# Seven half-size products for the latent tokens in the first layer's feed-forward, and its residual added in DRAM

## The chip, the cores and the metric

The kernel runs on one core of one Trainium2 chip. The metric is the device time of one execution, in microseconds (us); the median over three runs is shown, and one execution was profiled.

## The reference

Two layers work on 512 latent tokens and 256 context tokens of 1024 features, in float32. Layer 0 has retention and mLSTM heads, layer 1 windowed attention. Each layer ends with a gated feed-forward of 2816 hidden columns; in layer 0 it runs for latent and context tokens with the same weights, in layer 1 for latent tokens alone:

```python
def _swiglu(h, w_in, w_out):
    g, u = jnp.split(h @ w_in, 2, axis=-1)
    return (jax.nn.silu(g) * u) @ w_out
...
        x = x + g1 * y
        x = x + g2 * _swiglu(_rmsnorm(x, norm_w[layer, 1]) * (1.0 + sc2) + sh2, ffn_w_in[layer], ffn_w_out[layer])
        if not last:
            ctx = ctx + cg1 * yc
            ctx = ctx + cg2 * _swiglu(_rmsnorm(ctx, norm_w[layer, 1]) * (1.0 + csc2) + csh2,
                                      ffn_w_in[layer], ffn_w_out[layer])
```

The scales, shifts and gates (`sc2`, `sh2`, `g2` and so on) come from the conditioning vector through the matrices `ada_w` (1024 x 6144 per layer).

## The kernel before

**Tiles.** Features lie on the 128 partitions, tokens along the free dimension: the residual stream `xt` is four tiles of two feature tiles by 768 tokens, context tokens 0 to 255 first and latent tokens 256 to 767 after them. A float32 product is made of three matmuls on numbers rounded for the fast path: high times high, high times low, low times high. So each weight tile is split into a high part (a cast on ScalarE) and a low part (a subtraction on VectorE), and each activation too.

**The feed-forward of layer 0** (`op_ffn`, L1505). `inproj` takes column tiles of 128 hidden columns, always one of the gate and one of the up half; I call these two a pair, and there are 22. Each pair needs 2 x 8 x 3 matmuls over the 512 latent tokens and as many over the 256 context tokens. ScalarE applies SiLU to the gate, VectorE multiplies, and the product is split again. After 6, 10, 14 and 18 pairs `outproj` (L1551) multiplies the oldest four with `ffn_w_out`; six are left for the end. Each of its eight output tiles is scaled by the gate and added to `xt` by one VectorE instruction per token part, straight from PSUM. The last group also sums squares for the next norm.

**The feed-forward of layer 1** (`op_ffn_seven`) is another one: the product of a pair is seen as a two by two block product (feature halves by token halves, gate and up as the two output rows) and is done in seven half-size products in place of eight, by sums of weight blocks (`Weights.seven`, L535, on VectorE) and sums of activation blocks (the forms t2, t3, n1, n4, in `norm_seven`); the first two pairs run plain. The results are put together by 256-wide VectorE instructions.

**Order of the work.** The program is written as Python generators. `Flow` (L28) runs them and keeps a rough clock per engine to decide in which order they emit instructions; the tile framework then schedules each engine's queue by that order and by what is ready in its own model. On the chip each queue runs in order. `Weights` (L482) loads weights through SyncE's queue three loads ahead, and splits them when a buffer is free. `ada_stream` (L691) multiplies rows of `ada_w` with the conditioning vector on VectorE (one instruction per row tile of 128 x 1024 and per column: latent, context) beside the main work; its loads stand in SyncE's queue too, in a ring of six buffers (`ada_open`, L738). Seven of these run beside the feed-forward of layer 0, one of them needed by its own output groups.

**Memory.** Nineteen large slots (`big`) are shared by all activations; PSUM has eight banks: two under the tag `mx`, two under `pj`, and two tiles of two banks each (`psum2`). Every instruction goes through the helper in L107, so the profile has one line and groups by tile name: `pg`, `pu` are gate and up products, `pf` outputs, `wr`, `wh`, `wl` weights as loaded, high and low, `aw` and `acc` rows and sums of the modulation.

## Time and profile before

| | us |
|---|---|
| median of 3 runs | 1776.29 (1775.38 to 1778.4) |
| profiled execution | 1777.82 |
| its span | 1776.0 |
| TensorE busy | 1721.4 (97%) |
| VectorE busy | 1136.9 (64%) |
| ScalarE busy | 685.5 (39%) |
| GpSimd busy | 274.6 (15%) |

The span is the time from the first to the last instruction of the profiled execution. The feed-forward of layer 0 lies between about 550 and 1107 us of it, that of layer 1 from about 1411 us to the end. Busy times of TensorE are those of pipelined matmuls, each shown longer than the time by which it moves the next one; the time of a matmul is therefore read from a row of many. The mean granted clock of TensorE was 0.985 of full speed. GpSimd issues no DMA in this kernel.

### The profile page before, as it was taken

To read this page: it belongs to the slowest core of one execution; us is meant where nothing else is said; L and a number is where in the kernel's file an instruction comes from. 1 tells how busy PE (TensorE), PEld (TensorE's weight loads), DVE (VectorE), ACT (ScalarE), POOL (GpSimd) and SP (SyncE) were. 2 spreads that over 40 slices of the span, in tenths; PEclk is the share of its full clock that TensorE was granted. 3 is DMA by queue.
4 is the path that set the end of the run, shared out by engine and by line. 5 is a ranking of instruction groups with operands and counts; after the bars stand their busy time and mean duration, and the time that the engine had idled before them with its cause. 6 is when DMAs were issued, how large, how long until landed. Compare 5 with 4: busy or idle time off the path is not lost.

```text
span 1776.0 us, 29522 instructions
## 1 busy us (share of the span) xinstructions
PE 1721.4 (97%) x11922; PEld 1528.9 (86%) x11922; DVE 1136.9 (64%) x2048; ACT 685.5 (39%) x1346; POOL 274.6 (15%) x271
## 2 busy tenths in 40 slices
PE   6899999999999999999999999898999999999998
PEld 5799899999878888888888888898666989999998
DVE  5845365756597376563544324869886687778785
ACT  4532344433325221212121123545776553444343
POOL 4211120201123000000000002426454300000000
PEclk8999899999999999999999999898999999999999
DMA  9511111011574264443542215322002623333335
GB/s 332 209 52 48 37 37 48 25 38 53 196 239 117 75 186 132 129 148 125 162 134 78 67 37 153 96 61 60 1 1 66 184 72 95 107 96 107 107 88 150
DMA packets 224556, 184.35 MB, mean 104 GB/s; under 512 B 7532, under 2 KB 206628, under 8 KB 224420
## 3 DMA queue, kind: packets, MB, share of 16 engines
q1 hardware_dynamic: 222468, 178.20, 32.9%
q10 hardware_dynamic: 1952, 4.27, 0.7%
q8 instruction: 94, 1.54, 0.4%
q14 instruction: 42, 0.34, 0.1%
HBM read 175.10 MB, written 7.34 MB: 103 GB/s over the span
## 4 chain that ended last, share of the span: by engine, by line
PE 84%; DVE 7%; ACT 3%; issue 3%; DMA 2%; POOL 1%; SPq 0%; POOLq 0%; ACTq 0%; DVEq 0%
PE pf L107 28%; PE pu L107 18%; PE pg L107 14%; PE pt L107 10%; PE sc L107 3%; PE ao L107 2%; PE mo L107 2%; PE atr L107 2%; PE ro L107 1%; DVE acc L107 1%; PE kv L107 1%; DVE wl L107 1%; PE me L107 1%; DMA wr<-in_ab_w_in_dram 1%; DVE hfull L107 1%
## 5 line engine op out<-in xcount | busy, mean ns | idle before, releaser
L107 ACT CAST wh<-wr 128x1024 fp32r<-128x1024 f32 (+1 forms) x186 | 188.2, 1012 | 345.7 <-PE pf L107 165.5
L107 DVE TENSOR_TENSOR wl<-wr,wh 128x1024 fp32r<-128x1024 f32 (+1 forms) x186 | 225.4, 1212 | 105.5 <-ACT wh L107 104.3
L107 POOL TENSOR_TENSOR nacc<-nacc,sq 128x256 f32<-128x256 f32 (+1 forms) x42 | 56.7, 1349 | 630.7 <-ACT sq L107 627.5
L107 DVE SCALAR_TENSOR_TENSOR xt<-pf,mod,xt 128x512 f32<-128x512 f32 (+1 forms) x160 | 97.7, 613 | 84.3 <-PE pf L107 83.8
L107 DVE TENSOR_TENSOR hfull<-pu,sq 128x512 f32<-128x512 f32 (+1 forms) x44 | 24.5, 557 | 149.9 <-PE pu L107 149.6
L107 PE MATMUL pf<-fh,wh 128*128 128x256 f32 (+1 forms) x352 | 119.3, 340 | 0.8 <-ACT wh L107 0.8
L107 PE MATMUL pf<-fl,wh 128*128 128x256 f32 (+1 forms) x352 | 118.5, 337 | 0.0
L107 PE MATMUL pf<-fh,wl 128*128 128x256 f32 (+1 forms) x352 | 118.0, 338 | 0.5 <-DVE wl L107 0.5
L107 PE MATMUL pf<-fu,wh 128*128 128x512 f32 (+1 forms) x448 | 116.2, 349 | 1.1 <-ACT fu L107 0.5
L107 PE MATMUL pu<-hT,wh 128*128 128x256 f32 x640 | 115.4, 280 | 0.0
L107 DVE SCALAR_TENSOR_TENSOR acc<-aw,cmod,acc 128x1024 f32<-128x1024 f32 x90 | 114.8, 1298 | 0.0
L107 PEld LDWEIGHTS pu<-hT,wh 128*128 128x128 f32 x640 | 97.8, 188 | 0.6 <-ACT hT L107 0.2
L107 PE MATMUL pu<-hT,wl 128*128 128x256 f32 x320 | 88.0, 281 | 1.4 <-DVE wl L107 1.4
L107 PE MATMUL pt<-wh,hh 128*128 128x256 f32 x288 | 84.2, 294 | 3.8 <-ACT hh L107 2.6
L107 PEld LDWEIGHTS pf<-fu,wh 128*128 128x128 f32 x448 | 76.8, 188 | 12.6 <-ACT fu L107 0.7
L107 PE MATMUL pt<-wl,hh 128*128 128x256 f32 x288 | 83.7, 292 | 0.0
L107 PE MATMUL pg<-g0h,wh 128*128 128x512 f32 (+1 forms) x220 | 82.1, 373 | 1.5 <-ACT sq L107 1.5
L107 POOL TENSOR_TENSOR aE<-aE,ast 128x512 f32<-128x512 f32 (+1 forms) x64 | 73.0, 1154 | 66.9 <-DVE ast L107 51.5
L107 PE MATMUL pg<-g0l,wh 128*128 128x512 f32 (+1 forms) x220 | 82.3, 374 | 0.0
L107 PE MATMUL pt<-wh,hl 128*128 128x256 f32 x288 | 82.2, 288 | 0.0
L107 PE MATMUL pu<-g0l,wh 128*128 128x512 f32 (+1 forms) x220 | 82.1, 373 | 0.0
L107 PE MATMUL pu<-g0h,wh 128*128 128x512 f32 (+1 forms) x220 | 81.9, 372 | 0.0
(382 smaller groups left out, 5169.2 us busy)
## 6 DMA issues: line engine op xcount, KB each, us to landing
wr<-in_ffn_w_in_dram SPq DMA_DIRECT2D x88, 512.0 KB, 3.9
aw<-in_ada_w_dram SPq DMA_DIRECT2D x84, 512.0 KB, 4.5
wr<-in_ab_w_in_dram SPq DMA_DIRECT2D x32, 512.0 KB, 4.3
wr<-in_ffn_w_out_dram SPq DMA_DIRECT2D x32, 512.0 KB, 4.7
wr<-in_ffn_w_out_dram SPq DMA_DIRECT2D x32, 384.0 KB, 3.6
wr<-in_ab_w_out_dram SPq DMA_DIRECT2D x16, 512.0 KB
wr<-in_attn_w_out_dram SPq DMA_DIRECT2D x16, 512.0 KB, 4.1
aw<-in_ada_w_dram SPq DMA_DIRECT2D x8, 768.0 KB
```

The source lines that it names most:

```text
L107: r = fn(*a, **k)
```

## The change

The latent tokens of 20 of the 22 pairs in layer 0 get the seven half-size products: per pair 7 x 4 x 3 matmuls of 256 columns. The context tokens keep their plain product, 48 matmuls of 256 columns, of which those with the gate stand after the first of the seven products, and those with the up half before the last two; both fill one bank of the tag `mx` (`bank_e`) that is read at the end of the pair. The first two pairs run plain, latent tokens in 256-wide halves. `Weights.seven` gets two more kinds of job: in `all` the up half is split whole and last, after the two sums.

The norm (`norm_seven0`) writes eight float32 tiles first, then splits them into the forms; b21, b12 and b22 wait until the outputs of the mixer are done, t2 to n4 until the context's norm is done. The forms take 12 large slots, so `xt` does not stay in SBUF: it is stored to `xs2` in DRAM, the four inner output groups are scaled by ScalarE into two halves of a staging tile and added in DRAM by accumulating DMAs from GpSimd's queue, and `xt` is loaded again before the last group, which adds in SBUF as before. The groups now run after pairs 4, 8, 12 and 16 counted from 0. The modulation ring has three buffers in place of six, and the modulations stand after every third pair.

```diff
--- before.py
+++ after.py
...
-            yield lambda: self.asked > job[1] and "pool" in F1
+            F = F0 if job[2] in ("all", "eight0") else F1
+            yield lambda: self.asked > job[1] and "pool" in F
...
-            split("u", [t[:, 8:12] for t in x], u[:, 4:8])
-            self.freed += 2
-            self.ask()
-            yield
+            if job[2] == "seven":
+                split("u", [t[:, 8:12] for t in x], u[:, 4:8])
+                self.freed += 2
+                self.ask()
+                yield
             yield spend((self.n_p, 1))
             split("z", whl(), z)
             yield
             yield spend((self.n_p, 1))
             split("y", whl(), y)
+            if job[2] == "all":
+                yield
+                yield spend((self.n_x, 1))
+                split("u", xs_(), u)
+                self.freed += 2
+                self.ask()
...
-        pool_ = ada_ring["ctx"].enter_context(tc.tile_pool(name="aw", bufs=6))
+        pool_ = ada_ring["ctx"].enter_context(tc.tile_pool(name="aw", bufs=3))
-        for _ in range(6):
+        for _ in range(3):
             ada_ask()
...
+        F0["ctx"] = ExitStack()
+        F0["pool"] = F0["ctx"].enter_context(tc.tile_pool(name="f0", bufs=1))
+        F0["rows"], F0["sums"] = 8, 2
...
-    op_out(ab_w_out[0], mixed, 0, 2, (LAT, CTX), op_norm(0, 1, "g0"), (32, 24))
...
+    xs2 = drp.tile([4, P, 2 * NT], F32, name="xs2")
+    ORDER0 = ("b11", "b21", "b22", "", "", "t2", "t3", "n1", "n4")
...
+        for q in range(4):
+            bb.append(big([P, 3, NL], F32, "bb"))
+            for k in range(2):
+                kk = 2 * q + k
+                dve.scalar_tensor_tensor(bb[q][:, k], xk(xt, kk, a, b), amod[0][:, 1, kk, 0:1], bcs, ALU.mult, ALU.mult)
+                act.activation(bb[q][:, k], bb[q][:, k], AF.Identity, bias=mod[0][:, 24 + kk, 0:1])
...
+        for q, (b11, b21, b12, b22, t2) in enumerate(four):
+            two("b11", q, b11)
+        done0.add("b11")
+        yield lambda: "mixed" in done0
+        for name, i in (("b21", 1), ("b12", 2), ("b22", 3)):
+            for q in range(2):
+                two(name, q, four[q][i])
+            done0.add(name)
+            yield
+        yield lambda: 0 in done0
+        for q, (b11, b21, b12, b22, t2) in enumerate(four):
+            dve.tensor_tensor(b11, b11, b12, ALU.subtract)
+            dve.tensor_tensor(t2, b22, b11, ALU.add)
+        for name in ("t2", "t3", "n1", "n4"):
+            for q, (b11, b21, b12, b22, t2) in enumerate(four):
+                if name == "t3":
+                    dve.tensor_tensor(b12, b12, b22, ALU.subtract)
+                if name == "n4":
+                    dve.tensor_tensor(b21, b21, t2, ALU.subtract)
+                two(name, q, {"t2": t2, "t3": b12, "n1": b11, "n4": b21}[name])
+            done0.add(name)
+            yield
...
+    def norms0(part):
+        def run():
+            flow.add(norm_seven0() if part is LAT else norm_ctx0(), 3, "norm")
+            if part is CTX:
+                done0.add("mixed")
+                for kk in range(4):
+                    nc.gpsimd.dma_start(xs2[kk], xt[kk].rearrange("p j n -> p (j n)"))
+        op_do(run)
+
+    op_out(ab_w_out[0], mixed, 0, 2, (LAT, CTX), norms0, (32, 24))
+
...
+        def product(o, w, r0, name, start=True):
+            wh, wl = w
+            pairs = []
+            for k in range(4):
+                h, lo = form0(0, name, k // 2)[:, k % 2], form0(1, name, k // 2)[:, k % 2]
+                pairs += [(wh[:, r0 + k], h), (wh[:, r0 + k], lo), (wl[:, r0 + k], h)]
+            for i, (l_, r_) in enumerate(pairs):
+                pe.matmul(o, l_, r_, start=(start and i == 0), stop=(i == 11), skip_group_check=True)
...
+        def inproj(fi):
             def gen():
-                th, tl = big([P, 2, NT], F32R, "fh"), big([P, 2, NT], F32R, "fl")
-                acts[pr] = th, tl
...
-                for t in range(2):
...
-                        for j in range(2):
-                            if len(u) <= j:
-                                u += yield from W.take(1)
-                                ps.append([bank("pg") for _ in range(2)] if j == 0 else halves_ps(psum2("pu")))
-                            yield from steps(ps[j][i][:, 0:b - a], pairs_feat(u[j], 0, *x_(), a, b), cut=24)
-                            if part is (ends if first else parts)[-1]:
-                                W.give(1)
-                            if j:
-                                evac(t, part, ps[0][i], ps[1][i])
-                            flow.cur.t = 0.0
-                            yield
...
+                acts[fi] = t = big([P, 2, NT], F32R, "fu")
+                u, = yield from W.take(1)
+                keep = F0["pool"].tile([P, NL], F32, tag="keep", name=nm("keep"), bufs=2)
+                u23 = F0["pool"].tile([P, 2, 256], F32, tag="u23", name=nm("u23"), bufs=1)
+                m1 = keep[:, 256:512]
+
+                def context(i):
+                    yield from steps(bank_e[:, 256 * i:256 * i + 256], pairs_feat(u["gu"[i]], 0, ctx0(0), ctx0(1), 0, NCX),
+                                     cut=24)
+
+                bank_a = psum("pg", "mx")[:, 0:256]
+                product(bank_a, u["g"], 0, "b11")
+                act.copy(m1, bank_a)
+                rest()
+                yield
+                bank_e = psum("pc", "mx")
+                yield from context(0)
+                rest()
+                yield
+                product(bank_a, u["g"], 4, "b21", start=False)
+                W.n_x.n += 1
+                act.activation(keep[:, 0:256], bank_a, AF.Silu)
+                rest()
+                yield lambda: "z" in u and "t2" in done0
+                pu = psum2("pu")
+                bank_b, bank_d = pu[:, 0:256], pu[:, 512:768]
+                product(bank_b, u["z"], 0, "t2")
+                dve.tensor_tensor(u23[:, 0], bank_b, m1, ALU.subtract)
+                rest()
+                yield lambda: "y" in u and "t3" in done0
+                product(bank_d, u["y"], 0, "t3")
+                dve.tensor_tensor(u23[:, 1], bank_d, u23[:, 0], ALU.add)
+                rest()
+                yield lambda: "n1" in done0
+                bank_c = bank("pu")[:, 0:256]
+                product(bank_c, u["y"], 4, "n1")
+                W.give(1)
+                cc = t3("hfull")
+                dve.tensor_tensor(cc[:, 256:512], u23[:, 1], bank_c, ALU.subtract)
+                rest()
+                yield lambda: "u" in u
+                yield from context(1)
+                rest()
+                yield lambda: "n4" in done0
+                product(bank_d, u["u"], 4, "n4", start=False)
+                W.n_x.n += 1
+                dve.tensor_tensor(cc[:, 0:256], bank_d, u23[:, 0], ALU.add)
+                rest()
+                yield
+                product(bank_c, u["z"], 4, "b22", start=False)
+                W.give(1)
+                dve.tensor_tensor(m1, bank_c, u23[:, 0], ALU.subtract)
+                act.activation(m1, m1, AF.Silu)
+                dve.tensor_tensor(cc, cc, keep, ALU.mult)
+                act.copy(t[:, 0, NCX:NT], cc)
+                dve.tensor_tensor(t[:, 1, NCX:NT], cc, f(t[:, 0, NCX:NT]), ALU.subtract)
+                rest()
+                yield
+                output(fi, slice(0, NCX), bank_e[:, 0:256], bank_e[:, 256:512])
...
+        def output(fi, c, pg, pu):
...
+            act.activation(sg, pg, AF.Silu)
+            dve.tensor_tensor(cc, pu, sg, ALU.mult)
+            act.copy(t[:, 0, c], cc)
+            dve.tensor_tensor(t[:, 1, c], cc, f(t[:, 0, c]), ALU.subtract)
...
+        def plain():
...
+                for fi in range(PLAIN):
...
+                    for j in range(2):
+                        for r in range(2):
+                            for i, t in enumerate("gu"):
+                                yield lambda: halves[j][r] in done0
+                                product(banks[i][:, 256 * j:256 * j + 256], us[fi][t], 4 * r, halves[j][r], start=r == 0)
...
+                    acts[fi] = big([P, 2, NT], F32R, "fu")
+                    output(fi, slice(NCX, NT), *banks)
+                yield lambda: 0 in done0
...
+        def modulate(fi):
+            if ada and fi % 3 == 0:
                 l_, t0 = ada.pop(0)
-                op_ada(l_, t0, on_pe=(), gap=5.0 if l_ else 2.0, cols=1 if l_ and t0 >= 16 else 2)
+                op_ada(l_, t0, on_pe=(), gap=5.0 if l_ else 1.0, cols=1 if l_ and t0 >= 16 else 2)
...
+        def outproj(fs):
...
+                if not end and len(stage) == 0:
+                    stage.append(big([P, 2, NT], F32, "stage"))
...
                         for part in these:
                             a, b, mc = part
-                            ps = (bank if end and last else wide_bank)("pf")
+                            ps = wide_bank("pf")
                             yield from steps(ps[:, 0:b - a], pairs_feat(u, P * t, bh, bl, a, b, nk))
                             if part is these[-1] and t == ncol // P - 1:
                                 W.give(1)
-                            dve.scalar_tensor_tensor(xk(xt, k, a, b), ps[:, 0:b - a], mod[l][:, 40 + k, mc:mc + 1],
-                                                     xk(xt, k, a, b), ALU.mult, ALU.add)
+                            gate = mod[0][:, 40 + k, mc:mc + 1]
                             if end:
+                                dve.scalar_tensor_tensor(xk(xt, k, a, b), ps[:, 0:b - a], gate, xk(xt, k, a, b),
+                                                         ALU.mult, ALU.add)
+                                square_sum(k, a, b)
+                            else:
+                                act.activation(stage[0][:, k % 2, a:b], ps[:, 0:b - a], AF.Copy, scale=gate)
...
+                        if not end:
+                            nc.gpsimd.dma_start(xs2[k // 2, :, NT * (k % 2):NT * (k % 2) + NT], stage[0][:, k % 2],
+                                                accum_op=ALU.add)
...
             if end:
+                op_do(reload)
...
+        def reload():
+            nonlocal xt
+            xt = [big([P, 2, NT], F32, "xt") for _ in range(4)]
+            for kk in range(4):
+                nc.gpsimd.dma_start(xt[kk].rearrange("p j n -> p (j n)"), xs2[kk])
+
+        for fi in range(NF):
+            if fi >= PLAIN:
+                inproj(fi)
+            elif fi == 0:
+                plain()
+            modulate(fi)
+            if fi % 4 == 0 and 0 < fi < NF - 4:
+                outproj(tuple(range(fi - 4, fi)))
+        outproj(tuple(range(NF - 6, NF)))
```

## Rows read from the trace of the kernel before

**Rows 1.** Windows view; columns: stretch, PE, PEld, DVE, ACT, POOL busy, clock, DMA
```profile
454.00:550.00 96.00, 94.03 (x582) 78.94 (x581) 78.61 (x90) 38.81 (x58) 25.57 (x17) 1.00 0.71 225
550.00:690.00 140.00, 138.47 (x799) 119.85 (x798) 85.42 (x111) 38.33 (x58) 5.91 (x6) 1.00 0.40 117
690.00:1060.00 370.00, 370.00 (x2125) 318.44 (x2124) 175.26 (x223) 73.71 (x109) 0.00 (x0) 1.00 0.36 112
1060.00:1107.00 47.00, 46.19 (x253) 39.68 (x252) 19.79 (x27) 16.95 (x25) 10.32 (x9) 1.00 0.46 137
```

**Rows 2.** Waits view, 563 to 1107 us: total, times, longest
```profile
PE pg L107 <- ACT sq L107: 1.5, 1, 1.5
```

**Rows 3.** Chain of waits in order of time, first layer: start, us, what
```profile
604.25 4.89 PE pg L107 x21
609.14 5.59 PE pu L107 x24
...
618.26 2.84 PE pu L107 x24
621.10 4.88 PE pg L107 x21
```

**Rows 4.** Chain of waits, second layer's feed-forward
```profile
1629.16 7.07 PE pu L107 x60
```

**Rows 5.** Groups by form, VectorE, 563 to 1107 us: busy, mean ns, idle before
```profile
L107 DVE SCALAR_TENSOR_TENSOR acc<-aw,cmod,acc 128x1024 f32<-128x1024 f32 x70 | 87.8, 1276 | 0.0
L107 DVE TENSOR_TENSOR wl<-wr,wh 128x1024 fp32r<-128x1024 f32 x57 | 69.7, 1222 | 40.1 <-ACT wh L107 39.8
L107 DVE SCALAR_TENSOR_TENSOR xt<-pf,mod,xt 128x512 f32<-128x512 f32 x40 | 30.0, 750 | 46.5 <-PE pf L107 46.4
...
L107 DVE TENSOR_TENSOR hfull<-pu,sq 128x512 f32<-128x512 f32 x22 | 15.2, 691 | 130.6 <-PE pu L107 130.5
...
L107 DVE TENSOR_SCALAR acc<-aw,cmod 128x1024 f32<-128x1024 f32 x10 | 7.3, 744 | 0.1
```

**Rows 6.** Groups by form, VectorE, 1410 to 1776 us (second layer)
```profile
L107 DVE TENSOR_TENSOR ws<-ws,wr 128x512 f32<-128x512 f32 x40 | 27.3, 683 | 0.3
...
L107 DVE TENSOR_TENSOR u<-pu,m 128x256 f32<-128x256 f32 x20 | 8.3, 416 | 0.2
```

**Rows 7.** Windows view, second layer's feed-forward: its start, a steady stretch
```profile
1420.00:1430.00 10.00, 7.42 (x50) 7.43 (x51) 8.93 (x19) 6.09 (x12) 1.14 (x1) 0.83 0.03 8
...
1540.00:1600.00 60.00, 60.00 (x413) 55.48 (x412) 48.10 (x72) 24.74 (x36) 0.00 (x0) 1.00 0.32 97
```

**Rows 8.** Chain of waits where the first feed-forward begins
```profile
550.08 0.47 PE pu L107 x2
550.54 2.33 PE pg L107 x10
...
562.04 1.28 ACT L107
...
563.98 8.36 PE pg L107 x45
```

**Rows 9.** Instructions in order of time, VectorE, before that beginning
```profile
539.98 1.40 DVE L107 SCALAR_TENSOR_TENSOR hfull<-xt,amod,nbc 128x512 f32<-128x512 f32 x2
...
550.24 0.47 DVE L107 SCALAR_TENSOR_TENSOR xt<-pf,mod,xt 128x256 f32<-128x256 f32 x1
```

**Rows 10.** DMA issues: count, KB each, median us to landing
```profile
aw<-in_ada_w_dram SPq DMA_DIRECT2D x84, 512.0 KB, 4.5
...
wr<-in_ffn_w_out_dram SPq DMA_DIRECT2D x32, 384.0 KB, 3.6
...
xt<-xs SPq DMA_DIRECT2D x4, 768.0 KB, 8.8
```

**Rows 11.** Instructions in order of time, VectorE, second layer: one latent chain's ends
```profile
1644.38 0.41 DVE L107 TENSOR_TENSOR sq<-pu,u 128x256 f32<-128x256 f32 x1
...
1648.15 0.69 DVE L107 TENSOR_TENSOR fu<-hfull,fu 128x512 fp32r<-128x512 f32 x1 [0.69 <-ACT fu L107]
```

More of the change, by code (lines that the diff above doesn't have):

```diff
@@ L494, in plan @@
                 i = len(self.todo)
-                if sp[0] in ("seven", "eight"):
+                if sp[0] in ("seven", "eight", "all", "eight0"):
                     self.todo += sp[1:]
@@ L554, in sums, with xs_ @@
             def sums():
-                return F1["pool"].tile([P, KT, P], F32, tag="ws", name=nm("ws"), bufs=3)
-            x = [F1["pool"].tile([P, 12, P], F32R, tag=t, name=nm(t), bufs=2) for t in ("xh", "xl")]
+                return F["pool"].tile([P, KT, P], F32, tag="ws", name=nm("ws"), bufs=F["sums"])
+            def xs_():
+                return [F["pool"].tile([P, F["rows"], P], F32R, tag=t, name=nm(t), bufs=2) for t in ("xh", "xl")]
+            x = xs_()
             split("g", [t[:, 0:8] for t in x], g)
@@ new lines, in ctx0, with norm_seven0, two @@
+    def ctx0(lo):
+        return lambda k, a, b: piece0(12 + 4 * lo + k // 2)[:, k % 2]
+    def norm_seven0():
+        a, b, mc = LAT
+        ps2 = psum("nsum")
+        for i in range(a // P, b // P):
+            pe.matmul(ps2[:, i:i + 1], nacc[:, P * i:P * i + P], cst[:, C_INV:C_INV + 1], start=True, stop=True)
+        bcs = yield from rms_bc((ps2[:, a // P:b // P], a // P))
+        yield lambda: {(0, 24 + t) for t in (0, 4, 8, 12)} <= ada_done
+        bb = []
+        def two(name, q, src):
+            h, lo = form0(0, name, q), form0(1, name, q)
+            act.copy(h, src)
+            dve.tensor_tensor(lo, src, f(h), ALU.subtract)
+        for q in range(4):
[4 more added lines that the diff above has]
+                act.activation(bb[q][:, k], bb[q][:, k], AF.Identity, bias=mod[0][:, 24 + kk, 0:1])
+        four = [(bb[q][:, 0:2, 0:256], bb[2 + q][:, 0:2, 0:256], bb[q][:, 0:2, 256:512], bb[2 + q][:, 0:2, 256:512],
+                 bb[q][:, 2].rearrange("p (k n) -> p k n", k=2)) for q in range(2)]
+        for q, (b11, b21, b12, b22, t2) in enumerate(four):
[20 more added lines that the diff above has]
+            yield
@@ L1554, in outproj @@
             ncol = 256 if nk == 4 else P
[L1555 to L1558 removed]
+            end = fs[-1] == NF - 1
+            bh = lambda k, a, b: acts[fs[k]][:, 0, a:b]
+            bl = lambda k, a, b: acts[fs[k]][:, 1, a:b]
+            specs = [(ffn_w_out[0, r0:r0 + P * nk, ncol * s:ncol * s + ncol], nk, ncol) for s in range(D // ncol)]
@@ L1837, in reload1 @@
         F1["pool"] = ctx.enter_context(tc.tile_pool(name="f1", bufs=1))
+        F1["rows"], F1["sums"] = 12, 3
         xt = [big([P, 3, NL], F32, "xt") for _ in range(3)]
@@ L2013, in place @@
             acts[fi] = res
-        def columns(fi):
-            return tuple(wfeat(ffn_w_in[1, :, c:c + P]) for c in (P * fi, DFF + P * fi))
         PLAIN = 2
@@ L2098, in outproj @@
                 op(lambda: gen((LAT,)), specs)
-        op(plain, [("eight",) + columns(fi) for fi in range(PLAIN)])
+        op(plain, [("eight",) + columns(1, fi) for fi in range(PLAIN)])
         for fi in range(PLAIN, NF):
```

114 lines of the change are left out of this document (62 added, 52 removed).

## The prediction

> **What bounds the kernel now.** I read the windows view first, over the stretches around the first layer's feed-forward [rows 1]. From 550 to 1107 us TensorE is busy for 554.7 of 557 us at full clock, and in the long middle for 370.00 of 370. VectorE has 280 us of work there and ScalarE 129. The waits of that stretch hold one wait of TensorE, of 1.5 us, on ScalarE's table load and SiLU [rows 2]. So the stage lasts as long as its matmuls, and less matmul work is worth its full length as long as nothing else becomes late. The chain of waits, in order of time, gives the price of a matmul [rows 3]: 24 of 512 columns take 5.59 us (0.233 each), 24 of 256 columns 2.84 us (0.118 each), and one pair of column tiles (gate and up, latent and context) takes 621.10 - 604.25 = 16.85 us, which is 48 x 0.233 + 48 x 0.118. A 256-column matmul thus costs 0.508 of a 512-column one, so halving the width loses little.
>
> **The products.** A pair now has 2 x 8 x 3 = 48 matmuls of 512 columns for the latent tokens. After the change it has 7 products of 4 x 3 = 84 matmuls of 256 columns, and the 48 for context stay. In the second layer, which already works so, 60 such matmuls take 7.07 us [rows 4], 0.118 each. The new pair: (84 + 48) x 0.118 = 15.58 us, 1.27 less; over 20 pairs 25.4 us. The two plain pairs run 96 of 256 columns in place of 48 of 512: 11.33 against 11.18, 0.3 us more for both. Output products are the same, in groups 4, 4, 4, 4, 6. Net on TensorE: -25.1 us.
>
> **VectorE's new work.** Four weight splits of 1.22 us [rows 5] per pair in place of two, four sums at 0.68, five 256-wide additions at 0.42 [rows 6], two 256-wide context steps at the same price, and two 512-wide steps at 0.69 [rows 5]: 4.88 + 2.73 + 2.92 + 1.38 = 11.9 us per pair of 15.6 us. The modulation columns add 70 x 1.276 + 10 x 0.744 = 96.8 us over the stage as before. Over four pairs and their output group (62.3 + 8 x 4.2 = 96 us) VectorE needs 47.7 + 4 x 1.22 + about 18 = 71 us, 74%, and up to 84% while a two-column modulation runs. A steady stretch of the second layer has 48.10 us of VectorE in 60 (80%) beside 60.00 of TensorE [rows 7], so this load was carried once without a stall. There the pair is prepared about one pair ahead; here too (two buffers for the gate and up parts, three for the sums), so a lateness of some us does not reach TensorE. Four groups of output sums leave VectorE for ScalarE (32 x 0.75 and more [rows 5]); that is 8 us per group on an engine with 129 of 557 us filled. I take 2 us for the steady part: below nothing it cannot go (TensorE has no idle time to win back), and its other end is the second rival.
>
> **The start of the stage.** Before, the first pair's matmuls follow the norm tile by tile: TensorE begins at 550.1, in the middle of VectorE's norm steps, and stands still only from 561 to 564 [rows 8]. After, all eight norm tiles come before the first half-size form, and the weights' splits and the context part's residuals stand in the same queue. From the first norm step at 539.98 [rows 9] VectorE has 8 x 0.73 + 2 x 0.69 for the first form, four residual steps of 0.47 and six splits of 1.22: 16.4 us at most, 9 without the splits that can wait. The form is there at 549 to 556, while the context output ends at 550. So 0 to 6 us of standing still in place of 3; I take 5, +2 net. Three modulation buffers in place of six: VectorE takes 2 x 1.276 us for each row of two columns [rows 5], and such a row of 512 KB lands in 4.5 us [rows 10], so three rows in flight nearly suffice; 0 to 4 us later, I take 1. The stall may also cost clock: with 7.42 of 10 us busy the granted clock was 0.83 at the second layer's start [rows 7], some 1.7 us; I take 1. The store of x and the forms for t2 to n4 have 34 us of plain products over them (2 x 16.85), against 33 us of VectorE work. Start in all: +4, between -3 and +11.
>
> **The residual by DMA.** Each output tile of the four inner groups is scaled by ScalarE into one of two halves of a staging tile, and 32 accumulating DMAs of 384 KB, issued from GpSimd, add it in DRAM. No row shows such a DMA. The nearest below is a plain load of 384 KB, 3.6 us to landing; the nearest above is a load of 768 KB, 8.8 us [rows 10], since an accumulation moves the bytes more than once. One output tile takes TensorE 12 x 0.233 + 12 x 0.118 = 4.2 us, so a half is due again after 8.4 us; it is held for the context part (1.4), about 0.5 of ScalarE (an estimate by the 256-wide steps of rows 6), and the DMA. Below 6.5 us nobody waits. At 8.8 each second tile is 2.3 us late, 6.9 per group, of which four PSUM banks hide about 5.6: 1.3 x 4 = 5 us. Behind the waiting ScalarE instruction stand the weight casts, then VectorE's splits, then TensorE. I take 5.5 us for the DMA, nearer to the row with its own bytes, and a cost of 1. GpSimd has nothing else to do there (0.00 busy in 690 to 1060 [rows 1]).
>
> The Trainium skill (DMA: Bandwidth & Descriptors, Anatomy of one DMA) gives a GpSimd-issued DMA about 2.0 us plus the bytes over 436 GB/s, which is 2.9 us here, an estimate; by it this term would be 0. Its measured base is plain copies, and the 3.6 us row is already above it.
>
> **The reload.** x comes back in four GpSimd DMAs of 768 KB before the last group. One slot of the 19 is free early (12 forms, 6 activations), three more when the last pair's first forms are used up, some 8 us before that pair ends; with 8.8 us to landing they arrive about when the last group begins, and x tile 1 is needed two output tiles of 18 x 0.233 later. Cost 0 to 6, I take 1.
>
> **Sum.** -25.1 + 2 + 4 + 1 + 1 = -17 us. The profiled execution took 1777.8 us (span 1776.0 and 1.8 around it), so 1760.7; the median of the runs is 1.5 lower, 1776.3, which gives 1759 to 1760. **Forecast 1760 us.**
>
> **Rivals.** (1) *Nothing is lost*: start and DMAs are covered, 1752. For it: TensorE's 370.00 of 370. Against: the form that needs all eight norm tiles.
> (2) *VectorE falls behind beside the modulation.* In four successive pairs (62 us) it needs 47.7 us, and a two-column modulation adds 19.4 within about three pairs: 67 of 62. There are three such (the other four are half as long); 5 us late each, less what the prefetch covers and the output group gives back, is 8 to 12 more: 1769.
> (3) *The context bank, and the kernel is slower.* The context products of a pair stay in one PSUM bank until after the latent chain; the next pair's first product uses the other bank of that tag, and the product after it is context again and needs this one. In the second layer the chain after a pair's last product lasted from 1644.38 to 1648.84, 4.5 us [rows 11]; two more reads (0.8) come after it. With 1.4 us of product between, TensorE would wait 3.9 us per pair in the written order, 2.5 if the second gate product moves ahead: 20 x 2.5 = 50, 1810. It decides at a release later than the products that the scheduler can put ahead of the context's. Against it: the PE queue is not in written order. The program writes 24 gate matmuls and then 24 up; the trace has 2 up, 10 gate and so on [rows 8], so what is ready is put in front, and five products (7 us) are ready here. An idle of that size would also show in the clock [rows 7]. The Trainium skill (TensorE: Matmul & The Clock Gate, Part 1) says that the engine is throttled by default and activity releases it; by that a wait in every pair would run some matmuls at 1.2 GHz and make this rival longer still, and the 0.83 row agrees.
> (4) *The accumulation is slow.* From about 9.8 us per DMA (3 x 3.3 - 5.6 = 4.3 per group, 17 in all) the gain is gone; at 12 us it costs 44, 1804. For it: three passes over the bytes beside weight loads. Against: the 3.6 us row.
>
> **Chances.** The forecast (1755 to 1767) 0.50, rival 1 0.13, rival 2 0.14, rival 3 0.10, rival 4 0.09 (a quarter of it still faster), other 0.04. Times within 0.2% (3.6 us) cannot be told from no change. Faster: 0.50 + 0.13 + 0.14 + some 0.01 = 0.78; same 0.06, where small losses of rivals 2 and 4 meet; slower 0.16. The range of 1751 to 1783 leaves out the upper part of rivals 3 and 4 (0.15) and a little below (0.03); the likeliest case alone has 1755 to 1767.
>
> **What would show it.** Right: a pair's period of 15.6 us in the chain, TensorE still at 97% or more between 560 and the end of the stage, staging DMAs landing under 6.5 us and no wait of ScalarE on them, the stage's end near 1085. Wrong: waits of TensorE on the context bank's readers or on weight splits, granted clock under 1.00 in the stage, ScalarE waiting for the accumulations, or a pause between the last pair and its outputs where x is not back.

## The result: 0.9% slower, and the profile after

The changed kernel takes 1792.4 us (median of 4 runs, 1790.8 to 1796.1), beside 1777.1 for the kernel before on the same chip: ratio 1.009, 95% interval 1.0071 to 1.0108. The forecast was 1760, faster; it was wrong in sign. The profiled execution has a span of 1789.0 us against 1776.0.

The windows view of the kernel after, over the stretches of [rows 1] (columns as there):

```profile
454.00:550.00 96.00, 91.65 (x542) 75.62 (x541) 76.70 (x88) 34.92 (x51) 20.34 (x15) 0.98 0.67 210
550.00:600.00 50.00, 47.54 (x400) 47.08 (x399) 44.14 (x71) 28.29 (x50) 6.94 (x7) 1.00 0.38 117
600.00:630.00 30.00, 18.46 (x134) 15.84 (x133) 28.07 (x35) 7.80 (x12) 0.00 (x0) 0.83 0.52 158
630.00:670.00 40.00, 33.13 (x248) 31.57 (x247) 33.16 (x41) 13.84 (x21) 0.00 (x0) 0.94 0.52 157
670.00:700.00 30.00, 29.44 (x167) 24.30 (x166) 10.90 (x15) 9.74 (x16) 6.15 (x7) 0.96 0.73 143
700.00:1000.00 300.00, 297.07 (x2236) 280.17 (x2236) 193.87 (x266) 117.38 (x187) 20.84 (x24) 1.00 0.60 154
1000.00:1060.00 60.00, 57.97 (x477) 57.69 (x476) 42.48 (x62) 22.28 (x35) 1.46 (x2) 0.97 0.41 116
```

The products themselves do what was computed. The chain of waits in a late pair, in order of time, answers to [rows 3]:

```profile
1046.75 2.84 PE pu L107 x24
1049.59 1.18 PE pg L107 x10
1050.77 1.40 PE pu L107 x12
...
1062.24 0.83 PE pu L107 x7
```

A pair takes 1062.24 - 1046.75 = 15.5 us (15.58 forecast, 16.85 before), and from 700 to 1000 us TensorE is nearly full again. But between 600 and 630 it is busy for 18 of 30 us, with VectorE at 28 of 30. TensorE's waits from 454 to 1122 us (total, times, longest) answer to [rows 2]:

```profile
PE pu L107 <- ACT wh L107: 9.6, 2, 9.1
PE pf L107 <- ACT stage L107: 6.7, 3, 4.8
PE pf L107 <- DVE xt L107: 4.0, 3, 2.4
PE pu L107 <- DVE u L107: 3.0, 2, 2.0
PE pu L107 <- DVE g L107: 2.1, 1, 2.1
PE pf L107 <- DVE keep L107: 2.1, 1, 2.1
```

(The waits on xt and on g lie before 560 us, in the mixers' outputs and at the start of the stage.) The longest one, of 9.1 us, in VectorE's instructions in order of time: two rows of the modulation (acc, two columns, 2.47 us each) stand among the four weight sums (ws) of a pair.

```profile
612.90 0.68 DVE L107 TENSOR_TENSOR ws<-wr,wr 128x512 f32<-128x512 f32 x1
...
615.56 2.47 DVE L107 SCALAR_TENSOR_TENSOR acc<-aw,cmod,acc 128x1024 f32<-128x1024 f32 x2
617.96 0.41 DVE L107 TENSOR_TENSOR fu<-hfull,fu 128x256 fp32r<-128x256 f32 x1
618.29 0.68 DVE L107 TENSOR_TENSOR ws<-ws,wr 128x512 f32<-128x512 f32 x1
618.89 0.41 DVE L107 TENSOR_TENSOR keep<-pu,u 128x256 f32<-128x256 f32 x1
619.23 2.46 DVE L107 SCALAR_TENSOR_TENSOR acc<-aw,cmod,acc 128x1024 f32<-128x1024 f32 x2
621.62 0.68 DVE L107 TENSOR_TENSOR ws<-ws,wr 128x512 f32<-128x512 f32 x1
```

The last sum ends at 622.3; only then can ScalarE cast it, and only then does TensorE go on, 9.1 us late (ScalarE's row, in order of time):

```profile
622.38 1.05 ACT L107 CAST wh<-ws 128x1024 fp32r<-128x1024 f32 x1 [2.63 <-DVE ws L107]
```

TensorE's row, in order of time:

```profile
623.48 0.79 PE L107 MATMUL pu<-g,wh 128*128 128x256 f32 x2 [9.11 <-ACT wh L107]
```

Standing still also cost clock. In the two windows of 10 us around the wait (columns as above) the granted clock is 0.88 and 0.61 on the mean, so part of them ran at the lower of the engine's two levels (1.2 of 2.4 GHz); the next 10 us, busy throughout, have 1.00 again.

```profile
610.00:620.00 10.00, 3.44 (x27) 3.04 (x26) 10.00 (x14) 1.23 (x3) 0.00 (x0) 0.88 0.49 145
620.00:630.00 10.00, 6.52 (x41) 4.90 (x42) 8.07 (x11) 2.31 (x4) 0.00 (x0) 0.61 0.43 142
630.00:640.00 10.00, 10.00 (x87) 10.00 (x86) 3.55 (x6) 3.28 (x5) 0.00 (x0) 1.00 0.19 55
```

To say where the time went, the matmuls that begin in a stretch are priced at full clock (0.233 us for 512 columns, 0.118 for 256, as in [rows 3], narrower ones in proportion) and taken from its length. What remains is lost TensorE time: waits and clock together. It is good to 1 or 2 us per stretch: eight of the modulation's own small sums (tile ada) take 0.57 us and are priced at 0.94, so a full stretch can come out below zero. "Stage end" is the first norm-sum matmul behind the last latent output. All columns but the last are from the profiled executions; that of e10 lies 6 us above its median, those of e3, e4, e9 and e11 lie some 3 to 4 us below theirs. The ratio is to the kernel before, with its 95% interval.

| kernel | 500-600 | 600-700 | 700-1000 | 1000-1100 | stage end | median us, ratio |
|---|---|---|---|---|---|---|
| before | 4.2 | -0.7 | -1.4 | -0.3 | 1102.4 | 1777 |
| after | 10.2 | 25.0 | 3.0 | 4.4 | 1117.4 | 1792.4, 1.0090 (1.0071-1.0108) |
| e1 one column | 10.9 | 12.8 | 3.6 | 2.2 | 1099.9 | 1775.2, 0.9996 (0.9986-1.0006) |
| e2 no accumulation | 10.9 | 23.4 | 0.2 | 0.4 | 1110.5 | 1786.6, 1.0055 (1.0040-1.0070) |
| e3 first rows only | 14.3 | 7.2 | 6.2 | 1.9 | 1104.2 | 1783.3, 1.0043 (1.0028-1.0058) |
| e4 spread | 10.7 | 14.1 | 9.8 | 1.6 | 1109.9 | 1792.3, 1.0089 (1.0071-1.0106) |
| e5 beside outputs | 12.0 | 24.8 | 12.7 | 0.6 | 1125.5 | 1801.3, 1.0139 (1.0124-1.0154) |
| e6 e5, two DMAs | 10.2 | 24.7 | 14.4 | 1.2 | 1125.8 | 1803.3, 1.0150 (1.0135-1.0165) |
| e7 e6, GpSimd | 13.6 | 25.6 | 12.2 | 4.8 | 1128.8 | 1806.3, 1.0177 (1.0156-1.0199) |
| e8 plain write | 12.2 | 24.4 | 0.3 | 0.4 | 1111.0 | 1785.5, 1.0047 (1.0031-1.0063) |
| e9 four plain | 10.0 | 16.9 | 5.9 | 0.3 | 1109.6 | 1787.6, 1.0048 (1.0033-1.0063) |
| e10 early | 12.6 | 6.8 | 5.4 | 4.8 | 1107.4 | 1780.5, 1.0020 (1.0008-1.0033) |
| e11 early, late | 12.0 | 0.1 | 12.9 | 1.2 | 1099.6 | 1778.2, 1.0004 (0.9995-1.0014) |
| e12 mixers | 13.6 | 0.2 | 6.5 | 3.2 | 1095.8 | 1772.1, 0.9974 (0.9965-0.9983) |
| e13 mixers, later | 13.8 | 0.5 | 4.8 | 2.8 | 1098.2 | 1773.2, 0.9981 (0.9970-0.9992) |
| e14 before, moved | 4.1 | -0.7 | -1.2 | 0.0 | 1101.4 | 1779.9, 1.0018 (1.0009-1.0027) |
| e15 e12, plain write | 13.9 | 0.0 | 1.3 | 4.2 | 1091.3 | 1767.6, 0.9944 (0.9931-0.9957) |

After against before: 40.8 us more lost (42.6 - 1.8) set against 25.1 us of matmuls saved gives 15.7; the stage end moved by 15.0. Nearly two thirds of the loss lie in 600 to 700.

### The profile page after: what moved, and what is told of

Same layout as the page of the kernel before. It is cut to its first block, busy times and chain, and to the rows that moved or that the text cites. A ratio compares the mean times of both kernels' runs of the same rounds, so it can differ in the third digit from the quotient of the medians.

```text
span 1789.0 us, 31618 instructions
## 1 busy us (share of the span) xinstructions
PE 1705.2 (95%) x12738; PEld 1552.5 (87%) x12738; DVE 1241.6 (69%) x2224; ACT 773.7 (43%) x1502; POOL 300.6 (17%) x307
## 3 DMA queue, kind: packets, MB, share of 16 engines
q0 software_dynamic: 5760, 18.88, 5.4%
## 5 line engine op out<-in xcount | busy, mean ns | idle before, releaser
L107 PE MATMUL pf<-fu,wh 128*128 128x512 f32 (+1 forms) x1152 | 292.6, 345 | 10.8 <-ACT stage L107 6.7
L107 PEld LDWEIGHTS pf<-fu,wh 128*128 128x128 f32 x1152 | 197.5, 189 | 40.8 <-ACT stage L107 7.9
L107 PE MATMUL pf<-fu,wl 128*128 128x512 f32 (+1 forms) x576 | 196.4, 343 | 1.0 <-DVE wl L107 1.0
L107 PE MATMUL pu<-g,wh 128*128 128x256 f32 x704 | 130.8, 283 | 10.6 <-ACT wh L107 9.6
L107 DVE TENSOR_TENSOR wl<-ws,wh 128x1024 fp32r<-128x1024 f32 x80 | 97.1, 1218 | 56.9 <-ACT wh L107 47.8
L107 PE MATMUL pc<-g,xh 128*128 128x256 f32 x672 | 122.2, 281 | 0.9 <-ACT stage L107 0.9
L107 PEld LDWEIGHTS pf<-fu,wl 128*128 128x128 f32 x576 | 108.8, 189 | 15.7 <-DVE wl L107 1.7
L107 PEld LDWEIGHTS pu<-g,wh 128*128 128x128 f32 x704 | 108.8, 190 | 12.4 <-ACT wh L107 10.2
L107 DVE TENSOR_TENSOR xl<-wr,xh 128x1024 fp32r<-128x1024 f32 x84 | 91.4, 1093 | 25.3 <-ACT xh L107 25.1
L107 PEld LDWEIGHTS pc<-g,xh 128*128 128x128 f32 x672 | 103.4, 189 | 1.5 <-ACT stage L107 1.1
L107 PE MATMUL pu<-g,wl 128*128 128x256 f32 x352 | 99.2, 283 | 0.0
```

Source lines behind the costliest of these rows:

```text
L107: r = fn(*a, **k)
```

## The experiments

Theory A: VectorE is overfilled where the two-column modulations lie beside the first pairs. B: the backlog of the stage's start delays those pairs. C: the accumulating DMAs hold ScalarE, and ScalarE the weight casts.

**e1, one column.**

```diff
-op_ada(l_, t0, on_pe=(), gap=5.0 if l_ else 1.0, cols=1 if l_ and t0 >= 16 else 2)
+op_ada(l_, t0, on_pe=(), gap=5.0 if l_ else 1.0, cols=1)
```

> Left out: the context column of the first three modulations (10 us of VectorE each); every DMA stays. The changed kernel loses about 24 us of TensorE between 600 and 700 us. Theory A (VectorE is overfilled by the two-column modulations put beside the first pairs): the loss there falls to 8 us or less, the time to 1776 +- 4. Theory B (the backlog of the stage's start, norm forms and context residuals, is what delays the first pairs, and the modulation only stands beside it): 5 us less at most, 1787 or more. Theory C (ScalarE and the staging half wait for the accumulating DMAs): no change, 1792.

1775.2 us: A's time. The loss of 600 to 700 falls from 25.0 to 12.8 us, by half and not to A's 8; the stage ends 17.5 us earlier. What is left at 600 to 630 is TensorE waiting once, 4.8 us, for the modulation's own sum in its queue; at the first output group, behind 650, it waits 4.4 us on ScalarE.

**e2, no accumulation**, takes the whole statement out; **e8, plain write**, is this:

```diff
-nc.gpsimd.dma_start(xs2[k // 2, :, NT * (k % 2):NT * (k % 2) + NT], stage[0][:, k % 2],
-                    accum_op=ALU.add)
+nc.gpsimd.dma_start(xs2[k // 2, :, NT * (k % 2):NT * (k % 2) + NT], stage[0][:, k % 2])
```

> Left out: the 32 accumulating DMAs (the residual of the four inner groups never reaches DRAM; ScalarE still scales every tile into the staging tile, x is still stored and loaded back). Theory A: only TensorE's direct waits on the staging tile go, 6.7 us with what clock they cost: 1784 to 1788. Theory C: ScalarE's 51 us of waiting delayed weight casts and so the pairs; 15 us or more come back, 1777 or less. Theory B: as A.

> Left out: the addition. The 32 staging DMAs write in place of accumulating, all else is as in the changed kernel. It prices the accumulation: if moving the bytes more than once is what makes a staging DMA land after 5.9 us, a plain write lands in about 3.6 to 4 us and the time is that without the DMAs, 1784 to 1788. If the GpSimd queue is what costs, the landing stays above 5 us and the time near 1792.

1786.6 and 1785.5: not C, but 6 to 7 us that the forecast had put at 1. The time lies in A's range, but A's reason is not the one: of the 6.7 us of direct waits 4.6 to 4.8 stay (below), and what comes back lies after 700 us, where the loss falls from 7.4 to 0.6 and 0.7 us. The DMA issues of the kernel after (count, KB each, median us to landing):

```profile
xs<-stage POOLq DMA_DIRECT2D x32, 384.0 KB, 5.9
```

The same row of e8:

```profile
xs<-stage POOLq DMA_DIRECT2D x32, 384.0 KB, 3.5
```

With plain writes the whole cost is gone, so it is the addition's 2.4 us per DMA and not the GpSimd queue. Both times the profile counts the same 18.88 MB for that queue, but their packets took 5.4% of the 16 DMA engines' span with the addition and 2.8% without. The Trainium skill (DMA: Bandwidth & Descriptors, Anatomy of one DMA) gives a GpSimd-issued DMA 2.0 us plus the bytes over 436 GB/s, 2.9 us for this size, an estimate; the plain write's 3.5 is near it, the accumulating one's 5.9 is not.

The 4.8 us wait "PE pf <- ACT stage" in the first output group stays in both: it is not a DMA. TensorE's waits from 560 to 1125 us (total, times, longest) of e2:

```profile
PE pf L107 <- ACT stage L107: 4.6, 1, 4.6
```

And of e8:

```profile
PE pf L107 <- ACT stage L107: 4.8, 1, 4.8
```

ScalarE's rows after show it:

```profile
660.38 0.42 ACT L107 ACTIVATE keep<-keep 128x256 f32<-128x256 f32 x1 [0.42 <-DVE keep L107]
665.64 0.62 ACT L107 CAST fu<-hfull 128x512 fp32r<-128x512 f32 x1 [4.84 <-DVE hfull L107]
666.17 1.05 ACT L107 ACTIVATE stage<-pf,mod 128x512 f32<-128x512 f32 x2
```

The scaling of the first output tile stands behind a cast that waits for VectorE, which has the second modulation among its pair work. The Trainium skill (PSUM — Partial Sum Buffer, Engine vs sequencer instructions) says that ScalarE's and VectorE's queues are strictly first in, first out; these rows agree.

**e3, first rows only**, in the modulations of this stage:

```diff
-                for i in range(cols):
+                for i in range(cols if k < rows else 0):
...
-op_ada(l_, t0, on_pe=(), gap=5.0 if l_ else 1.0, cols=1 if l_ and t0 >= 16 else 2)
+op_ada(l_, t0, on_pe=(), gap=5.0 if l_ else 1.0, cols=1 if l_ and t0 >= 16 else 2, rows=1)
```

> Left out: of each of the seven modulations of this stage the multiplications of rows 2 to 8 (some 88 us of VectorE); every DMA, the transposes and the final sums stay. It shows the stage with the new products and DMAs, without the modulation beside them. Theory A: what is left is the start and the DMAs, 6 + 7 us over the full gain: 1762 to 1768. Theory B: the first pairs are late all the same, 10 us or more of the 24 stay: 1774 or more. Theory C: 10 us or more stay too, with TensorE's waits named after the staging tile.

1783.3, a miss, and slower than e1 with more work. 600 to 630 is clean (TensorE 29.01 of 30 us), so B is out for that stretch. But the start lost 14.3 in place of 10.2, and TensorE waited 8.6 us on the staging tile, 4.5 of it at the first output group. That wait is neither the modulation's nor a staging DMA's: ScalarE, in order of time, stood for a weight.

```profile
653.16 1.05 ACT L107 CAST xh<-wr 128x1024 fp32r<-128x1024 f32 x1 [8.51 <-DMA wr<-in_ffn_w_in_dram]
```

The run is no clean test. Rows that nobody multiplies give their buffers back at once, so their loads follow each other as fast as they land: SyncE's queue, which loads the weights too, waited for them, and the pair's weight was issued only at 647.9, behind three of them. Its waits from 560 to 1110 us (total, times, longest); after has none by this name:

```profile
SPq L763 <- DMA aw<-in_ada_w_dram: 131.5, 39, 7.3
```

**e4, spread.**

```diff
-            if ada and fi % 3 == 0:
+            if ada and fi in (0, 6, 9, 12, 15, 18, 20):
...
-op_ada(l_, t0, on_pe=(), gap=5.0 if l_ else 1.0, cols=1 if l_ and t0 >= 16 else 2)
+op_ada(l_, t0, on_pe=(), gap=5.0 if l_ else 3.0, cols=1 if l_ and t0 >= 16 else 2)
```

> Nothing left out: the first modulation's rows are spaced at 3.0 in place of 1.0 in the planner, and the other six begin at column tiles 6, 9, 12, 15, 18 and 20 in place of 3, 6, 9, 12, 15 and 18. Theory A: the first modulation lies beside four pairs in place of two and the second away from them, so at least half of the 24 us goes: 1776 to 1782. Theory B: 1787 or more. Theory C: no change, 1790 or more.

1792.3, a miss. The spacing hardly took hold: the first modulation still ended at 627 us (625 after) and 14 us stayed at 600 to 650. The loss at the first output group went, and a new one of 6 us came at 800 to 850, where the third modulation now lies. The stage ended 7.5 us earlier, yet the median did not move: behind the stage this profile took 677.5 us, after's 671.6 (all kernels: 671.6 to 677.6). Why, was not traced.

**e5, e6, e7, modulations beside the output groups.** e5:

```diff
-            if ada and fi % 3 == 0:
+            for _ in range({0: 1, 4: 1, 8: 1, 12: 2, 16: 2}.get(fi, 0)):
...
-op_ada(l_, t0, on_pe=(), gap=5.0 if l_ else 1.0, cols=1 if l_ and t0 >= 16 else 2)
+op_ada(l_, t0, on_pe=(), gap=1.0 if l_ else 7.0, cols=1 if l_ and t0 >= 16 else 2)
```

e6 is e5 with the accumulating DMA inside the loop over parts, in place of the one behind it:

```diff
+nc.gpsimd.dma_start(xs2[k // 2, :, NT * (k % 2) + a:NT * (k % 2) + b], stage[0][:, k % 2, a:b], accum_op=ALU.add)
```

e7 is e6 with the low parts of the activations on GpSimd (here and in the same line of the latent chain):

```diff
-dve.tensor_tensor(t[:, 1, c], cc, f(t[:, 0, c]), ALU.subtract)
+pool.tensor_tensor(t[:, 1, c], cc, f(t[:, 0, c]), ALU.subtract)
```

> Nothing left out: the seven modulations lie elsewhere. A pair fills VectorE for 11.9 of 15.6 us, which leaves 24%, so a row of two columns (2.5 us) fits beside pairs each 10 us; beside an output group VectorE has nearly all of its 33 us. The first modulation gets 7.0 in place of 1.0 between its rows (it must end before the first output group); the second and third begin with the first and second output group, the four of one column with the third and fourth, by two. Theory A (two-column rows come faster than the share that pairs leave of VectorE; the place decides, not the sum): the 24 us of 600 to 700 fall to 8 or less, nothing new later: 1772 to 1778. Theory B (backlog from the stage's start): the loss at 600 to 630 stays, 1785 or more. Theory C (staging waits): what A wins comes out as longer waits on the staging tile, as without the modulation: 1780 to 1786.

> As the run with modulations beside the output groups, and each half of the staging tile is added by two accumulating DMAs, 256 KB for the latent and 128 KB for the context tokens, each issued once ScalarE has written its part; 64 in place of 32. Theory A: with VectorE no longer late, the staging waits (some 7 to 10 us) are the next loss; the latent part starts 1.4 us earlier and is shorter, so 4 to 8 us less than the run before it: 1766 to 1773. Theory that the cost of such a DMA is per DMA and not per byte (GpSimd needs 0.87 us to issue one): no gain or a loss of some us.

> As the run with two DMAs for each half, and the low parts of the activations (one 512-wide and one 256-wide subtraction a pair, 1.1 us of VectorE) are made by GpSimd, which takes 1.6 and 0.8 us for such steps and is idle there. Theory A: VectorE at 10.8 us of 15.6 a pair in place of 11.9; 0 to 4 us less than without it, 1764 to 1772. Rival: GpSimd's queue holds the accumulating DMAs, which wait for ScalarE; the low parts stand behind them, come late for the next output group and TensorE waits: slower than without it by 3 us or more.

1801, 1803 and 1806: all slower, and A missed three times; e6 and e7 came out as their rivals had it. With gap 7.0 the rows still came from 592 to 629 us (591 to 625 after): the gap acts in the planner's own time, and what stands on VectorE's queue hardly moved, so the loss of 600 to 700 stayed and these runs do not test A there. Beside the output groups the rows' loads met the accumulations. The DMA issues of e5:

```profile
xs<-stage POOLq DMA_DIRECT2D x32, 384.0 KB, 7.3
```

And of e6:

```profile
xs<-stage POOLq DMA_DIRECT2D x32, 256.0 KB, 6.8
xs<-stage POOLq DMA_DIRECT2D x32, 128.0 KB, 6.2
```

7.3 us is past the 6.5 from which the prediction let ScalarE wait, and TensorE waited 13.0 us on the staging tile (6.7 after). A third of the bytes lands only 1.1 us sooner, and splitting won nothing. In e7 GpSimd took 1.66 us for the 512-wide subtraction (VectorE 0.69), and TensorE's wait on weight casts grew from 11.4 to 16.6 us.

**e9, four plain pairs**, as two blocks of two:

```diff
-        PLAIN = 2
+        PLAIN = 4
...
-            elif fi == 0:
-                plain()
+            elif fi % 2 == 0:
+                plain((fi, fi + 1))
```

> Nothing left out: four plain pairs in place of two, as two blocks of two; the third and fourth column tile then need two weight splits in place of four and no sums. TensorE gets 2 x 1.27 = 2.5 us more work, VectorE some 14 us less before the first output group. Theory A (VectorE's queue is overfilled from 588 to 625 us): the 14 us lost between 600 and 650 fall to 4 or less, the loss at the first output group stays: 1781 to 1786. Theory that it is the place of the modulation's rows in the queue and not the sum of work: the loss stays, 1793 to 1796.

1787.6, 1.6 us above A's range. The loss of 600 to 650 fell from 14.5 to 4.8 and the waits on weight casts from 9.6 to 0.9, as A has it with less VectorE work in the same place; the first output group's loss stayed.

**e10, e11, the first modulation elsewhere.** It is started behind the one that the mixers' stage makes anyway, by `ada_stream(ada_turn[0], 0, 40, on_pe=(), gap=2.0, freed=1)`; e11 begins the other six by `fi in (6, 9, 12, 14, 16, 18)` besides.

```diff
                 op_ada_early()
+                op_ada_second()
...
-    op_ffn_first([(0, 40), (1, 8),
+    op_ffn_first([(1, 8),
```

> Nothing left out: the first modulation is made in the stage of the mixers, right behind the one that is made there already, on VectorE (24 to 38 of 50 us busy there), with its rows and sums in slots of that stage; the other six begin at column tiles 3, 6, 9, 12, 15 and 18 as in the changed kernel. Theory A: the 14 us lost between 600 and 650 fall to 2 or less; the 10 us at the first output group may grow by some us, since the pairs come to it earlier and the second modulation still begins at tile 3: 1777 to 1783. Theory B (the start's backlog): 1788 or more. Rival: the slots that the modulation takes delay the mixers, and the loss is found between 150 and 400 us.

> As the run with the first modulation among the mixers, and the other six begin at column tiles 6, 9, 12, 14, 16 and 18. Theory A: nothing but pairs on VectorE until the first output group, so the loss there falls too, to the 4 us that the run without multiplications showed: 1769 to 1776, faster than before. Theory C (the loss at the output group is the accumulating DMAs'): as without this step, 1777 or more.

1780.5 as A has it; 1778.2 a miss of A by 2 us. In e11 hardly anything is lost from 600 to 700 us (0.1) and 700 to 800 (0.9), first output group included, so that loss was the second modulation's and not C. Part of the gain went elsewhere: the moved modulation landed at 74 to 112 us, where VectorE was full already, and TensorE stood still there for 4 us more. The windows of e11:

```profile
60.00:100.00 40.00, 35.07 (x306) 30.38 (x305) 39.29 (x70) 17.27 (x27) 1.39 (x1) 1.00 0.58 204
100.00:150.00 50.00, 46.90 (x402) 43.53 (x402) 33.93 (x66) 13.53 (x26) 8.02 (x8) 1.00 0.21 58
```

The same windows of the kernel before:

```profile
60.00:100.00 40.00, 35.96 (x301) 31.91 (x301) 38.07 (x82) 20.91 (x35) 3.69 (x4) 0.91 0.33 109
100.00:150.00 50.00, 50.00 (x420) 47.56 (x419) 19.42 (x47) 10.93 (x22) 3.87 (x5) 1.00 0.22 60
```

Busy time alone misleads here, since before ran 60 to 100 at a granted clock of 0.91: priced like the table, e11's profiled execution has lost as much as before by 150 us (33.8 us both), while e10, at 0.89 and 0.94 in 100 to 112 and 112 to 150, has lost 36.8. In e11 a new loss of 7.2 came at 800 to 850, beside the second of the modulations that stay in the stage (792 to 826).

**e12, e13, the version that wins.** The first modulation runs later among the mixers, with its rows loaded then (e12: behind the second `ret_proj`, e13: behind the first `ml_proj`); the others start at tiles meant to lie clear of the losses seen.

```diff
+            yield from ada_stream(turn, 0, 40, on_pe=(), gap=5.0, freed=1)
...
+        else:
+            op_do(ada_second)
...
-        yield lambda: len(mh) == 4
+        yield lambda: len(mh) == 4 and (0, 44) in ada_done
...
-            if ada and fi % 3 == 0:
+            if ada and fi in (6, 10, 13, 15, 17, 19):
```

> Nothing left out: the first modulation is made on VectorE among the mixers, after the second retention projection (rows in two slots of that stage, loaded then), where VectorE is busy some 30 of 50 us; the other six begin at column tiles 6, 10, 13, 15, 17 and 19. If the place of the modulations is the cause (theory A): no loss from 600 to 1050 but the staging waits, none before 500: 6 us at the start and 4 to 7 on staging are left over the full gain, 1762 to 1768, faster than before. If the stage's own costs eat the gain: 1774 or more.

> As the run before it, with the first modulation one projection later (after the first of the two gated mixers' projections). Theory A: the same, 1762 to 1768. If any two-column modulation costs TensorE some us wherever it lies (its sums stand in TensorE's queue, its rows in VectorE's): 1770 or more, and the loss is found where it lies now, 200 to 300 us.

1772.1 and 1773.2: faster than both kernels, if by little (e12: 0.9974, interval 0.9965 to 0.9983), but 4 to 11 us short of what was expected, and e13 at the time of the theory that such a modulation costs wherever it lies. Priced like the table, TensorE lost 2.4 us more than before from 200 to 300 us in e12 (the rows lie at 198 to 248) and 5.3 more from 200 to 400 in e13 (276 to 312). The windows of e12:

```profile
500.00:600.00 100.00, 90.21 (x665) 82.19 (x665) 87.12 (x115) 45.26 (x73) 22.38 (x18) 0.97 0.55 174
600.00:950.00 350.00, 348.79 (x2635) 329.64 (x2634) 227.24 (x316) 138.28 (x218) 21.93 (x26) 1.00 0.54 134
950.00:1000.00 50.00, 46.06 (x329) 42.25 (x329) 26.49 (x37) 16.84 (x27) 6.52 (x8) 1.00 0.75 188
```

From 600 to 950 TensorE is full beside 65% of VectorE. What is left lies at the start (13.6 us) and at 950 to 1000 (4.5), where TensorE's waits are for ScalarE's scaling into the staging tile (2.3 and 1.0).

**e14, the control, and e15, the price of the addition in e12.** e14 is the kernel before with the first modulation moved as in e12; e15 is e12 without `accum_op`.

> The kernel before, with only the first modulation moved among the mixers as in the faster run; nothing left out. If the gain belongs to the seven products (theory A): TensorE had no loss beside that modulation here, so the move wins nothing and costs what it costs among the mixers, 2 to 4 us: 1777 to 1781. If the move itself is the gain: 1770 to 1774.

> The faster run (first modulation after the second retention projection) with staging DMAs that write in place of accumulating; left out is the addition. If what is left of the loss is the accumulation: the 4 us of 950 to 1000 and up to 3 more go, 1765 to 1768. If it is the start and the mixers: 1770 or more.

1779.9, the time that theory A gave, and 1767.6, in the range of "what is left is the accumulation". The move alone costs the kernel before 0.18% (0.09 to 0.27), so the gain of e12 is that of the changed feed-forward: by 500 us both have lost 100.0, and the stage ends at 1095.8 in place of 1101.4. The place where e14 should lose was not right, though: in its profile the stage ends 1.0 us earlier than before, and the time lies behind the stage (676.9 us for 673.6). The addition still costs 4.5 us in e12, and the loss of 950 to 1000 is gone without it (4.5 to -0.2).

## Why the prediction was wrong, by its own steps

- **The products, -25.1:** right. 15.5 us a pair; the matmuls up to the stage end, priced, are 998.1 us before and 973.0 after; the new VectorE steps cost what [rows 6] said (ws 684 ns, u 420); e12, with VectorE out of the way, carries it for 350 us.
- **VectorE's new work, +2: the step that failed.** It was sized as a mean, 74 to 84% over four pairs and their output group, and "a lateness of some us does not reach TensorE" was taken from a stretch of the second layer in which no modulation runs [rows 7]. Rival 2 had the mechanism, but at 5 us for each modulation less prefetch, 8 to 12 in all. The first modulation, which before lay at 620 to 652 us, came while VectorE was still splitting the forms (to 592 us) and before any lead had been built. Its first and last rows, and the last step of the forms (g), in VectorE's instructions in order of time:

```profile
590.65 1.41 DVE L107 TENSOR_SCALAR acc<-aw,cmod 128x1024 f32<-128x1024 f32 x2
591.98 0.68 DVE L107 TENSOR_TENSOR g<-bb,g 128x512 fp32r<-128x512 f32 x1
...
622.82 2.47 DVE L107 SCALAR_TENSOR_TENSOR acc<-aw,cmod,acc 128x1024 f32<-128x1024 f32 x2
```

  The windows view over it (columns as above) has VectorE busy throughout:

```profile
590.65:625.20 34.55, 23.01 (x181) 20.93 (x179) 34.55 (x44) 9.51 (x15) 0.00 (x0) 0.89 0.56 167
```

  It holds 1.41 + 7 x 2.47 = 18.7 us of the modulation, where pairs leave 24% of 34.5 us, 8.3. The 10.4 us too many answer to the waits of 600 to 630 (11.5), and with the clock 14.5 us were lost up to 650. The second one did it again at the first output group, through ScalarE's queue. From 600 to 700 that is 25.0 us in place of 2, of which e1 takes away half and e11 all. (Of the 25.0, e9 takes away 8 with the modulation left where it is and less pair work beside it: it is the sum in the queue that counts.)
- **Start, +4 (-3 to +11):** 10.2 - 4.2 = 6.0. Right in size. The wait for the first form is there (2.5 us for 1.5 before); the rest is 2.0 us more of waits on VectorE's xt additions and a granted clock of 0.83 at 530 to 540, which the forecast did not have. e8, which changes nothing there, has 2.0 us more, so such differences between runs say little. In e12 the loss is 9.4 above before; TensorE's waits on the xt additions are 7.0 us there, 4.0 after and 2.0 before; why VectorE comes later to them was not tested.
- **Accumulating DMA, +1:** the landing was near (5.9 for 5.5, against [rows 10]), the cost was not: 6.9 us by e2's stage end, 6.4 by e8's. "Below 6.5 us nobody waits" assumed that halves come due at an even 8.4 us. They do not. ScalarE's waits, 560 to 1110 us (total, times, longest):

```profile
ACT stage L107 <- DMA xs<-stage: 51.1, 19, 5.3
```

  And in e8, where a DMA lands after 3.5 us:

```profile
ACT stage L107 <- DMA xs<-stage: 22.0, 9, 4.8
```

  TensorE's own waits on the tile were 6.7 in all, 4.8 of them no DMA's. Most of the price comes later: after the last inner group a pair's sums begin late (1028.6 us), a step that TensorE needs stands behind them on VectorE, and that 2.0 us wait with its clock is gone in e2 (4.4 to 0.4 in 1000 to 1100).
- **Reload, +1:** no wait of TensorE names it.
- **Rival 3, the context bank:** did not happen; waits on that bank are 0.9 us in all. **Rival 4:** not at 5.9 us. The kernel is slower all the same, by rival 2 at two to three times its size plus the DMAs; none of the rivals on the slower side was the one that came. Three of the signs of "wrong" did: the granted clock under 1.00, ScalarE waiting for the accumulations, and waits of TensorE on weight casts.

Left open: why the start loses more in e12, and the 6 us by which the kernels differ behind the stage.

## What to carry to other kernels

When an engine takes on work, add up its queue between two dates, from the point where the previous stage lets it go to the first consumer, and not over a period: VectorE was busy for 68% of this stage (550 to 1117 us), and for all of the 35 us that decided. Side work that was free beside the old loop has to be placed anew, and its new place looked up in the busy time there: the same modulation came with a loss of 14 us at 600, of 0 to 3 net at 74 to 112 (VectorE 38 of 40 us busy before), of some 2 at 198 to 248 (32 of 50 us) and some 5 at 276 to 312. A planner's spacing is not the order on the engine; read the order from the trace.

## What the runs showed of the hardware

An accumulating DMA of 384 KB into DRAM landed after 5.9 us (median of 32), a plain write of the same shape from the same queue after 3.5. Beside the modulation's loads (e5) it was 7.3, and there 256 and 128 KB took 6.8 and 6.2 (e6), so in these runs the time was far from proportional to the bytes. GpSimd needed 0.87 us to issue one and 1.66 us for a 512-wide subtraction that VectorE does in 0.69.
